# Weights' low parts subtracted in pieces on GpSimd, and inverse norms left in PSUM, in a hybrid HGRN and attention layer

## The chip, the cores and the metric

The kernel runs on one core of a Trainium2 chip. The metric is the device time of one launch in microseconds (us). A core has TensorE (PE; its weight loads are listed as PEld), VectorE (DVE), ScalarE (ACT), GpSimd (POOL) and SyncE (SP), which issues the DMAs here. Each engine works through its own instructions in order and waits on semaphores for the others.

## The reference

One step of a layer in which two groups of heads work side by side, for a prompt of 2048 tokens and a sample of 32 tokens with a cache of 256. Cut to what matters:

```
h = rms_norm(x, norm1);  z = h @ w_in            # 1024 -> 3592 columns
# HGRN2: 4 heads of 128, chunks of 64
f = lb + (1 - lb) * sigmoid(fa);  k = 1 - f;  b = cumsum(log f)
o = (q*exp(b)) @ S0 + tril((q*exp(b-bref)) @ (k*exp(bref-b)).T) @ v
S = exp(b_last) * S0 + (k*exp(b_last-b)).T @ v
oa = rms_norm_per_head(o) * silu(ga)             # the "inverse norm of the HGRN output"
# FoX attention: 8 heads of 64
fq = rms_norm(qb, q_gain);  fk = rms_norm(kb, k_gain)   # the "inverse norm of Q"
p = softmax(fq @ fk.T / 8 + sum of log forget, causal);  ob = p @ v
x = x + concat(oa, ob) @ w_out
x = x + square(relu(rms_norm(x, norm2) @ w_up)) @ w_down
```

All of it is in float32.

## The kernel before

The prompt is worked on in four quarters of 512 tokens; the sample's 32 tokens ride with the third (544 columns, done as two of 272). A float32 product is made of three matmuls in a faster format: each operand is split into a high part (a rounded copy) and a low part (what is left), and high by high, high by low and low by high are summed in PSUM (`mm3`).

A weight comes in blocks of 128 x 1024 numbers, 384 of them in the launch. `load_w` loads one (L161, on SyncE), makes the high part `wh` on ScalarE (L163) and the low part `wl` on GpSimd (L165). Each of the three has two buffers. A strip of the projection is such a block of `w_in`; `strip` runs it over the quarters that are ready, and hands each result to an evacuation.

What happens between the strips is laid out at build time: `Flow` keeps a clock of the matmuls emitted and steps side jobs (generators) as their due times come, so that TensorE's order is a dense stream of strips with small jobs in between: `finish` of K, V and Q, the tails of HGRN, attention. A scheduler below the program places the instructions on their engines and adds the waits.

The steps that the change touches:

- `squares` puts the squares of x and their high and low parts into SBUF: product and subtraction on GpSimd (L287, L291), the copy on ScalarE (L289).
- In `fox_q`, `norm` sums them over the 64 rows of a head with two matmuls against ones (`tq`), in a PSUM tile of `ps_tr`. `inv_norm` makes exp(-0.5 ln(mean + eps)) with Ln (L279) and Exp (L280) into an SBUF tile, and VectorE multiplies Q by it and by the gain (L485). Ahead of L493 and L495, which split the result.
- In HGRN's `i_tail` the same is done for the output: matmuls (`th`), Ln (L762), Exp over all columns (L763), product on VectorE (L764). L790 to L794 follow in `g_tail`.
- `ps_tr` has two buffers, in turn. All transposes use it too: `ta` (activations), `tk`, `tv`, `th`, `mt`, `tg`, `tl`, `ts`.

Lines of VectorE that are named below and not changed: L247 (a row times its inverse norm and the gain), L429 and L430 (K times its inverse norm, times the gain), L634 to L647 (nine small products and copies that scale HGRN's queries and keys), L843 and L844 (high and low part of the attention's row maxima), L723 (the HGRN state), L883 (low part of attention weights, one operand in PSUM), L905, L916 and L920 (the end of a head's attention), L528 (the high part of V).

From some 1100 us on the kernel is in its second half: output projections, the second norm, and the feed-forward of one quarter after the other, with the attention of the later quarters beside it.

Of the kernel before, what the change touches and what calls it, by code (L numbers as in the profile page):

```python
# [9 lines left out]
F32 = mybir.dt.float32  # L10
# [3 lines left out]
AF = mybir.ActivationFunctionType  # L14
ALU = mybir.AluOpType
# [4 lines left out]
P = 128  # L20
# [55 lines left out]
def hymba_step(  # L76
# [8 lines left out]
    pe, act, dve, pool, sp = nc.tensor, nc.scalar, nc.vector, nc.gpsimd, nc.sync  # L85
# [8 lines left out]
    def mm(out, lhsT, rhs, start, stop):  # L94
        n = rhs.free_size()
        if rhs.dtype == F32:
            flow.t += max(n, 32) * 4 * 0.00042
        else:
            flow.t += n * 0.00042 if n >= 256 else 0.213
        pe.matmul(out, lhsT, rhs, start=start, stop=stop)  # L100

    def tp(out, in_, idn):
        flow.t += 0.109
        pe.transpose(out, in_, idn)  # L104
# [53 lines left out]
    def load_w(src, kt, ncols, pfx):  # L158

        raw = wpool.tile([P, kt, ncols], F32, tag="wraw", name=f"wr{pfx}", bufs=2)  # L160
        sp.dma_start(raw, src.rearrange("(k p) c -> p k c", p=P))  # L161
        hi = wpool.tile([P, kt, ncols], F32R, tag="whi", name=f"wh{pfx}")
        act.copy(hi, raw)  # L163
        lo = wpool.tile([P, kt, ncols], F32R, tag="wlo", name=f"wl{pfx}")
        pool.tensor_tensor(lo, raw, hi.bitcast(F32), op=ALU.subtract)  # L165
        return hi, lo

    def mm3(out, wh, wl, ah, al, kts):
# [10 lines left out]
    def nid():  # L179
        uid[0] += 1  # L180
        return uid[0]
# [93 lines left out]

    def inv_norm(ss, cnt):

        t = tt([P, 544])[:, 0:ss.free_size()]
        act.activation(t, ss, AF.Ln, scale=1.0 / cnt, bias=epsc)  # L279
        act.activation(t, t, AF.Exp, scale=-0.5)  # L280
        return t

    def squares(x):

        n = x.free_size()
        sq = tt([P, 544])[:, 0:n]
        pool.tensor_tensor(sq, x, x, op=ALU.mult)  # L287
        sh = tt([P, 544], F32R)[:, 0:n]
        act.copy(sh, sq)  # L289
        sl = tt([P, 544], F32R)[:, 0:n]  # L290
        pool.tensor_tensor(sl, sq, sh.bitcast(F32), op=ALU.subtract)  # L291
        return sh, sl
# [5 lines left out]
    def tt(shape, dt=F32, tag="t", bufs=None):  # L298
        return tmp.tile(shape, dt, tag=tag, name=f"{tag}{nid()}", bufs=bufs)

    def strip(col, A, qs, evac):
        hi, lo = load_w(w_in[:, col:col + P], KT, P, nid())
        for q in qs:
            ah, al = A[q]
            for c0, n in QCH[q]:
                ps = ps_mm.tile([P, 512], F32, tag="mm", name=f"mm{nid()}")
                yield from mm3(ps[:, 0:n], lambda k: hi[:, k, :], lambda k: lo[:, k, :],
                               lambda k: ah[:, k, c0:c0 + n], lambda k: al[:, k, c0:c0 + n],
                               [(k, k) for k in range(KT)])
                g = evac(q, c0, n, ps)  # L310
                if g is not None:
                    flow.spawn(g, SL)
                yield
# [253 lines left out]
    def hgrn(A, qs, h):  # L567
# [132 lines left out]
        def i_tail(q, d, z):  # L700
            vp = ps_tr.tile([P, 4, P], F32, tag="tr", name=f"th{nid()}")
            for i in range(4):
                tp(vp[:, i, :], z[:, i * P:(i + 1) * P], ident)
            v = tt([P, 544])
            act.copy(v[:, 0:512], vp.rearrange("p i k -> p (i k)"))
            v = v[:, 0:512].rearrange("p (i k) -> p i k", k=P)
            yield 1.0
            while "kt" not in d or (q > 0 and h_done[h] != q):
                yield 0.5
            kt_ = d["kt"][:, 0:512].rearrange("p (i k) -> p i k", k=P)  # L710
            up = ps_x.tile([P, 4, P], F32, tag="x", name=f"xu{nid()}")
            for i in range(4):
                mm(up[:, i, :], kt_[:, i, :], v[:, i, :], start=True, stop=True)
            us = tt([P, 544])[:, 0:512].rearrange("p (i k) -> p i k", k=P)
            act.copy(us, up)
            yield 0.3
            op = ps_x.tile([P, 4, P], F32, tag="x", name=f"xo{nid()}")
            QE, at, dec = d["QE"], d["at"], d["dec"]
            for i in range(4):
                mm(op[:, i, :], S_cur[h], QE[:, i * P:(i + 1) * P], start=True, stop=False)  # L720
                mm(op[:, i, :], v[:, i, :], at[:, i, :], start=False, stop=True)
                sn = tmp.tile([P, P], F32, tag=f"S{h}", name=f"S{h}_{nid()}", bufs=2)
                dve.scalar_tensor_tensor(out=sn, in0=S_cur[h], scalar=dec[:, i:i + 1], in1=us[:, i, :],  # L723
                                         op0=ALU.mult, op1=ALU.add)
                S_cur[h] = sn
                yield 0.6
            h_done[h] += 1
            at_busy[q % 2] = False
            o = tt([P, 544])
            act.copy(o[:, 0:512], op.rearrange("p i k -> p (i k)"))  # L730
            if q == 3:
                sp.dma_start(ns_p[0, 0, h], S_cur[h])
            if QN[q] > 512:
                yield 0.5
                ec = d["ec"]
                vp = ps_tr.tile([P, 512], F32, tag="tr", name=f"th{nid()}")
                tp(vp[0:TS, 0:P], z[:, 512:544], ident)
                vs = tt([TS, P], tag="vts", bufs=1)
                act.copy(vs, vp[0:TS, 0:P])
                s0 = tt([P, P], tag="s0", bufs=1)  # L740
                sp.dma_start(s0, state_hgrn[0, 0, h])
                yield 3.0
                xp_ = ps_x.tile([P, 512], F32, tag="x", name=f"xu{nid()}")
                mm(xp_[:, 0:P], d["kts"], vs, start=True, stop=True)
                mm(xp_[:, P:P + TS], s0, QE[:, 512:544], start=True, stop=False)
                mm(xp_[:, P:P + TS], vs, d["ats"], start=False, stop=True)
                sn = tt([P, P], tag="sn", bufs=1)
                dve.scalar_tensor_tensor(out=sn, in0=s0, scalar=ec[:, 2, 8:9], in1=xp_[:, 0:P],
                                         op0=ALU.mult, op1=ALU.add)
                sp.dma_start(ns_s[0, 0, h], sn)  # L750
                act.copy(o[:, 512:544], xp_[:, P:P + TS])

            n = QN[q]
            sh, sl = squares(o[:, 0:n])
            yield HLAT
            r = tt([P, 544])
            for c0, w in ((0, 512), (512, TS))[0:1 + (n > 512)]:
                c = slice(c0, c0 + w)
                ss = ps_tr.tile([P, 512], F32, tag="tr", name=f"th{nid()}")
                mm(ss[:, 0:w], oner, sh[:, c], start=True, stop=False)  # L760
                mm(ss[:, 0:w], oner, sl[:, c], start=False, stop=True)
                act.activation(r[:, c], ss[:, 0:w], AF.Ln, scale=1.0 / P, bias=epsc)  # L762
            act.activation(r[:, 0:n], r[:, 0:n], AF.Exp, scale=-0.5)  # L763
            dve.tensor_tensor(o[:, 0:n], o[:, 0:n], r[:, 0:n], op=ALU.mult)  # L764
            d["o"] = o

        def evac_g(q, c0, n, ps):
# [42 lines left out]
    cnt = {"kb0": 0, "kb1": 0, "qc": 0}  # L810
# [234 lines left out]
    def add_tokens(acc, ah, al, w, evac=None):  # L1045

        for hf in range(2):
            c = slice(512 * hf, 512 * hf + 512)
            hi, lo = load_w(w[:, c], 2, 512, nid())
            for t in range(4):  # L1050
                ts = slice(t * P, (t + 1) * P)
                ps = ps_mm.tile([P, 512], F32, tag="mm", name=f"mm{nid()}")
                yield from mm3(ps, lambda k: ah(k)[:, ts], lambda k: al(k)[:, ts],
                               lambda k: hi[:, k, :], lambda k: lo[:, k, :], [(0, 0), (1, 1)])
                dve.tensor_tensor(acc[:, t, c], acc[:, t, c], ps, op=ALU.add)  # L1055
                if evac is not None:
                    flow.spawn(evac(t, c), 1.5)
                yield
# [185 lines left out]
    epsc = const.tile([P, 1], F32, name="epsc")  # L1244
# [29 lines left out]
    for i in range(4):  # L1274
        t = const.tile([98, 512], F32R, name=f"kB{i}")
# [5 lines left out]
    for i in range(2):  # L1281
        t = const.tile([98, 512], F32R, name=f"qC{i}")
# [15 lines left out]
    for i in range(2):  # L1298
        t = tmp.tile([P, 4, P], F32, tag=f"AT{i}", name=f"AT{i}", bufs=1)
# [94 lines left out]
```

## Time and profile before

| | |
|---|---|
| time, median of 3 runs | 2978.21 us (2977.03 to 2981.14) |
| the profiled execution | 2982.22 us; span of its instructions 2980.5 us |
| mean granted TensorE clock | 0.990 |
| PE | busy 2875.0 us (96%), 15592 matmuls |
| DVE | busy 1840.9 us (62%), 3463 instructions |
| ACT | busy 1368.4 us (46%), 2391 instructions |
| POOL | busy 1091.2 us (37%), 600 instructions, of which L165 934.2 us |

Busy time of DVE and POOL counts from an instruction's start to its end, whatever it does in between. Matmuls overlap, so that a stall of TensorE is read better from the starts of consecutive matmuls than from its busy share.

### The profile page before, as it was taken

The page shows a single profiled execution, that of the slowest core. Times are in us where ns is not written, and L with a number is a line of the kernel's source. Part 1 is how long each engine was busy: PE and PEld are TensorE (multiplying, and loading weights), DVE is VectorE, ACT ScalarE, POOL GpSimd, SP SyncE. Part 2 cuts the span into 40 slices and gives each one's busy share as a digit, 9 for nine tenths or more (in the row PEclk, how much of TensorE's full clock was granted, in tenths as well). Part 3 has the DMA queues.
Part 4 walks back from the last instruction along what each step waited for, and adds up shares of the span by engine and source line. Part 5 has one row for each costly group of instructions (what it writes and reads, how often), then busy time and mean ns, then how long its engine had stood idle before and what let it go on. Part 6 is the DMA issues. An engine that isn't in the chain of part 4 may idle for free.

```text
span 2980.5 us, 42522 instructions
## 1 busy us (share of the span) xinstructions
PE 2875.0 (96%) x15592; PEld 2435.9 (82%) x15592; DVE 1840.9 (62%) x3463; ACT 1368.4 (46%) x2391; POOL 1091.2 (37%) x600
## 2 busy tenths in 40 slices
PE   6899999899999999999999999999999999999999
PEld 5777777877788878888888888978899989988887
DVE  6447778776876777766666666566666554444333
ACT  4445566655555554544444444454444433222232
POOL 5452233434112334433333333333333344344443
PEclk9899999999999999999999999999999999999999
DMA  5663344656433564344335633443633333243333
GB/s 163 186 187 87 102 121 117 179 156 186 116 102 89 162 202 128 110 121 119 114 123 156 189 112 112 130 141 111 185 108 109 93 103 93 86 129 107 96 95 99
DMA packets 464143, 381.86 MB, mean 128 GB/s; under 512 B 34928, under 2 KB 363904, under 8 KB 463936
## 3 DMA queue, kind: packets, MB, share of 16 engines
q1 hardware_dynamic: 463936, 379.15, 43.6%
q8 instruction: 123, 2.02, 0.3%
q14 instruction: 84, 0.69, 0.1%
HBM read 316.67 MB, written 62.40 MB: 127 GB/s over the span
## 4 chain that ended last, share of the span: by engine, by line
PE 62%; DVE 1%; ACT 1%; issue 0%; POOL 0%; DMA 0%; SPq 0%; DVEq 0%; ACTq 0%; POOLq 0%
PE mm L100 54%; PE ot L100 3%; PE st L100 3%; PE mx L100 1%; PE ta L104 0%; PE rs L100 0%; ACT wh L163 0%; DMA row<-X 0%; DVE acc L1055 0%; PE tx L104 0%; POOL wl L165 0%; PE ty L104 0%; DVE os L916 0%; DVE ml L920 0%; DVE row L247 0%
## 5 line engine op out<-in xcount | busy, mean ns | idle before, releaser
L165 POOL TENSOR_TENSOR wl<-wr,wh 128x1024 fp32r<-128x1024 f32 x384 | 934.2, 2433 | 1685.7 <-ACT wh L163 1483.0
L100 PE MATMUL mm<-ahi,wh 128*128 128x512 f32 (+1 forms) x2528 | 899.0, 356 | 2.9 <-ACT t L512 1.6
L100 PE MATMUL mm<-ahi,wl 128*128 128x512 f32 (+1 forms) x2528 | 884.9, 350 | 1.5 <-POOL wl L165 1.5
L100 PE MATMUL mm<-alo,wh 128*128 128x512 f32 (+1 forms) x2528 | 885.8, 350 | 0.0
L163 ACT CAST wh<-wr 128x1024 fp32r<-128x1024 f32 x384 | 403.5, 1051 | 745.0 <-PE mm L100 645.3
L100 PEld LDWEIGHTS mm<-ahi,wh 128*128 128x128 f32 x2528 | 481.0, 190 | 63.2 <-DVE t L621 2.6
L100 PEld LDWEIGHTS mm<-ahi,wl 128*128 128x128 f32 x2528 | 479.7, 190 | 62.2 <-POOL wl L165 1.9
L100 PEld LDWEIGHTS mm<-alo,wh 128*128 128x128 f32 x2528 | 480.9, 190 | 57.3 <-issue 0.5
L1055 DVE TENSOR_TENSOR acc<-acc,mm 128x512 f32<-128x512 f32 x480 | 326.1, 683 | 155.7 <-PE mm L100 150.1
L879 ACT ACTIVATE st<-st 128x512 f32<-128x512 f32 (+1 forms) x320 | 169.3, 529 | 351.1 <-PE st L100 188.7
L883 DVE TENSOR_TENSOR pl<-st,ph 128x512 fp32r<-128x512 f32 (+1 forms) x320 | 198.2, 620 | 198.0 <-ACT ph L881 196.6
L100 PE MATMUL mm<-wh,uh 128*128 128x512 f32 x768 | 306.9, 400 | 2.8 <-DVE acc L1055 1.6
L100 PE MATMUL mm<-wh,ul 128*128 128x512 f32 x768 | 302.7, 395 | 0.0
L100 PE MATMUL mm<-wl,uh 128*128 128x512 f32 x768 | 302.5, 394 | 0.0
L1115 DVE TENSOR_TENSOR mm<-mm,r 128x512 f32<-128x512 f32 (+1 forms) x160 | 95.8, 599 | 291.0 <-ACT r L1114 289.1
L839 DVE TENSOR_REDUCE mc<-mx 128x1 f32<-128x512 f32 (+2 forms) x320 | 195.7, 617 | 36.9 <-PE mx L100 34.5
L100 PEld LDWEIGHTS mm<-wh,uh 128*128 128x128 f32 x768 | 144.6, 188 | 41.3 <-DVE acc L1055 7.5
L100 PEld LDWEIGHTS mm<-wh,ul 128*128 128x128 f32 x768 | 144.8, 189 | 35.2 <-DVE ul L1117 0.2
L887 DVE TENSOR_TENSOR acc<-acc,st 128x512 f32<-128x512 f32 (+2 forms) x288 | 173.3, 602 | 0.0
L881 ACT CAST ph<-st 128x512 fp32r<-128x512 f32 (+1 forms) x320 | 169.8, 532 | 7.2
L100 PEld LDWEIGHTS mm<-wl,uh 128*128 128x128 f32 x768 | 144.8, 189 | 30.8
L100 PE MATMUL mm<-uh,wh 128*128 128x272 f32 x512 | 149.6, 292 | 1.3 <-DVE acc L1148 1.3
(296 smaller groups left out, 4275.6 us busy)
## 6 DMA issues: line engine op xcount, KB each, us to landing
wr<-in_w_up_dram SPq DMA_DIRECT2D x128, 512.0 KB
wr<-in_w_down_dram SPq DMA_DIRECT2D x128, 512.0 KB
wr<-in_w_in_dram SPq DMA_DIRECT2D x96, 512.0 KB
kB<-KS SPq DMA_DIRECT2D x160, 128.0 KB
kA<-KS SPq DMA_DIRECT2D x80, 256.0 KB
V<-VS SPq DMA_DIRECT2D x80, 256.0 KB
wr<-in_w_out_dram SPq DMA_DIRECT2D x32, 512.0 KB
out_dram<-t SPq DMA_DIRECT2D x32, 256.0 KB
```

The source lines that it names most:

```text
L100: pe.matmul(out, lhsT, rhs, start=start, stop=stop)
L163: act.copy(hi, raw)
L165: pool.tensor_tensor(lo, raw, hi.bitcast(F32), op=ALU.subtract)
L839: dve.tensor_reduce(out=mc[:, j, kb:kb + 1], in_=mx[:, 0:n], axis=AX.X, op=ALU.max)
L879: act.activation(st[:, off:], st[:, off:], AF.Exp)
L881: act.copy(ph[:, off:], st[:, off:])
L883: dve.tensor_tensor(pl[:, off:], st[:, off:], ph.bitcast(F32)[:, off:], op=ALU.subtract)
L887: dve.tensor_tensor(acc[:, off:], acc[:, off:], st[:, off:], op=ALU.add)
L1055: dve.tensor_tensor(acc[:, t, c], acc[:, t, c], ps, op=ALU.add)
L1115: dve.tensor_tensor(z, z, r, op=ALU.mult)
```

## The change

The subtraction that makes a weight's low part is done in four instructions of 256 columns each instead of one of 1024; its operands are seen as flat rows of 1024. `inv_norm` writes its Ln and Exp over the sums, in the PSUM tile where the matmuls left them, and returns that tile; `norm` multiplies Q by it from there. The HGRN output's norm calls `inv_norm` too, for each range of columns (512, and in the third quarter another 32), and multiplies each range by the PSUM tile.

```diff
@@ load_w
         act.copy(hi, raw)
         lo = wpool.tile([P, kt, ncols], F32R, tag="wlo", name=f"wl{pfx}")
-        pool.tensor_tensor(lo, raw, hi.bitcast(F32), op=ALU.subtract)
+
+        fl = lambda a: a.rearrange("p k c -> p (k c)")
+        for c in range(0, kt * ncols, 256):
+            s = slice(c, c + 256)
+            pool.tensor_tensor(fl(lo)[:, s], fl(raw)[:, s], fl(hi.bitcast(F32))[:, s], op=ALU.subtract)
         return hi, lo
@@ inv_norm
-        t = tt([P, 544])[:, 0:ss.free_size()]
-        act.activation(t, ss, AF.Ln, scale=1.0 / cnt, bias=epsc)
-        act.activation(t, t, AF.Exp, scale=-0.5)
-        return t
+        act.activation(ss, ss, AF.Ln, scale=1.0 / cnt, bias=epsc)
+        act.activation(ss, ss, AF.Exp, scale=-0.5)
+        return ss
@@ i_tail
-            r = tt([P, 544])
             for c0, w in ((0, 512), (512, TS))[0:1 + (n > 512)]:
                 c = slice(c0, c0 + w)
                 ss = ps_tr.tile([P, 512], F32, tag="tr", name=f"th{nid()}")
                 mm(ss[:, 0:w], oner, sh[:, c], start=True, stop=False)
                 mm(ss[:, 0:w], oner, sl[:, c], start=False, stop=True)
-                act.activation(r[:, c], ss[:, 0:w], AF.Ln, scale=1.0 / P, bias=epsc)
-            act.activation(r[:, 0:n], r[:, 0:n], AF.Exp, scale=-0.5)
-            dve.tensor_tensor(o[:, 0:n], o[:, 0:n], r[:, 0:n], op=ALU.mult)
+                r = inv_norm(ss[:, 0:w], P)
+                dve.tensor_tensor(o[:, c], o[:, c], r, op=ALU.mult)
```

## Rows read from the trace of the kernel before

**Rows 1.** Busy us of each engine, granted clock and DMA, in two stretches.
```profile
core 0: us, PE busy (x) PEld busy (x) DVE busy (x) ACT busy (x) POOL busy (x), PEclk, DMA share, GB/s
0.00:1200.00 1200.00, 1104.96 (x6176) 915.26 (x6177) 847.24 (x1691) 661.89 (x1273) 419.31 (x289) 0.98 0.50 143
1200.00:2981.00 1781.00, 1770.03 (x9417) 1520.66 (x9415) 993.65 (x1773) 706.51 (x1118) 671.85 (x311) 1.00 0.40 118
```

**Rows 2.** Four VectorE lines: duration ns min/median/max, first and last start us, forms.
```profile
L485 DVE SCALAR_TENSOR_TENSOR t<-t,qg,t x20: 215/746/2960, 74.6 to 773.0; 128x512 f32<-128x512 f32 x16, 128x32 f32<-128x32 f32 x4
...
L429 DVE TENSOR_TENSOR t<-t,krs x20: 281/1174/2883, 46.0 to 742.9; 128x512 f32<-128x512 f32 x16, 32x128 f32<-32x128 f32 x4
...
L634 DVE COPY hcc<-he x16: 150/160/2361, 222.6 to 1052.2; 128x4 f32<-128x4 f32 x16
...
L883 DVE TENSOR_TENSOR pl<-st,ph x320: 391/681/693, 247.9 to 2394.0; 128x512 fp32r<-128x512 f32 x128, 128x256 fp32r<-128x256 f32 x32
```

**Rows 3.** Timeline about 600 us: start us, us, instruction [idle before <- ended by].
```profile
599.32 2.39 POOL L165 TENSOR_TENSOR wl<-wr,wh 128x1024 fp32r<-128x1024 f32 x1 [2.03 <-ACT wh L163]
...
599.73 2.52 DVE L485 SCALAR_TENSOR_TENSOR t<-t,qg,t 128x512 f32<-128x512 f32 x1
...
601.20 0.29 PE L100 MATMUL mm<-alo,wh 128*128 128x272 f32 x1
602.91 0.38 PE L100 MATMUL mx<-kB,qC 96*128 96x256 f32 x1 [1.42 <-DVE mc L839]
```

**Rows 4.** Timeline of TensorE: the first and the last of 59 stalls.
```profile
28.24 0.42 PE L100 MATMUL mm<-alo,w 128*40 128x512 f32 x1 [0.35 <-DVE alo L198]
...
1153.27 0.47 PE L100 MATMUL mm<-wh,ahi 128*128 128x512 f32 x1 [1.42 <-DVE acc L1055]
```

**Rows 5.** Stretches of low clock, first and last of ten; columns as in rows 1.
```profile
74.70:81.60 6.90, 5.58 (x15) 4.55 (x16) 3.72 (x8) 2.66 (x5) 0.00 (x0) 0.51 0.84 246
...
1037.30:1040.70 3.40, 3.40 (x13) 2.81 (x12) 2.73 (x9) 2.03 (x4) 0.00 (x0) 0.50 1.04 249
```

**Rows 6.** Two GpSimd lines; columns as in rows 2.
```profile
L165 POOL TENSOR_TENSOR wl<-wr,wh x384: 2340/2403/3459, 24.1 to 2965.5; 128x1024 fp32r<-128x1024 f32 x192
...
L291 POOL TENSOR_TENSOR t<-t,t x32: 1266/1302/1843, 55.7 to 1080.2; 128x512 fp32r<-128x512 f32 x24, 128x544 fp32r<-128x544 f32 x8
```

**Rows 7.** GpSimd's lines by shape: busy us, mean ns, idle before and its releasers.
```profile
L165 POOL TENSOR_TENSOR wl<-wr,wh 128x1024 fp32r<-128x1024 f32 x384 | 934.2, 2433 | 1685.7 <-ACT wh L163 1483.0 <-PE st L100 49.7 <-PE ot L100 33.4
L291 POOL TENSOR_TENSOR t<-t,t 128x512 fp32r<-128x512 f32 x24 | 32.5, 1356 | 18.6 <-ACT t L289 17.9 <-DMA KS<-t 0.7
```

**Rows 8.** Timeline of the feed-forward stage: a subtraction and the first load of its result.
```profile
2709.77 2.42 POOL L165 TENSOR_TENSOR wl<-wr,wh 128x1024 fp32r<-128x1024 f32 x1 [3.96 <-ACT wh L163]
...
2714.22 0.19 PEld L100 LDWEIGHTS mm<-ahi,wl 128*128 128x128 f32 x1
```

**Rows 9.** Waits: engine and line <- what ended them: us in total, times, longest.
```profile
PE mm L100 <- POOL wl L165: 2.7, 2, 1.5
...
ACT wh L163 <- DMA wr<-in_w_in_dram: 8.6, 4, 3.4
```

**Rows 10.** Timeline of GpSimd and VectorE at three places where their instructions meet.
```profile
24.13 5.70 POOL L165 TENSOR_TENSOR wl<-wr,wh 128x1024 fp32r<-128x1024 f32 x2
...
24.20 3.39 DVE L247 SCALAR_TENSOR_TENSOR row<-row,rs,gbc 128x1024 f32<-128x1024 f32 x1
...
364.25 3.40 POOL L165 TENSOR_TENSOR wl<-wr,wh 128x1024 fp32r<-128x1024 f32 x1 [1.82 <-ACT wh L163]
...
364.74 0.68 DVE L641 TENSOR_TENSOR t<-t,hcc 128x512 f32<-128x512 f32 x1
...
1055.09 2.56 POOL L165 TENSOR_TENSOR wl<-wr,wh 128x1024 fp32r<-128x1024 f32 x1
...
1055.34 2.85 DVE L641 TENSOR_TENSOR t<-t,hcc 128x512 f32<-128x512 f32 x1
```

**Rows 11.** Timeline about 565 us: a norm of Q and the next transposes.
```profile
564.89 0.69 ACT L279 ACTIVATE t<-tq,epsc 128x512 f32<-128x512 f32 x1
...
565.71 0.60 PE L104 MATMUL tk<-identr,t 128*128 128x128 f32 x4
...
567.29 0.74 DVE L485 SCALAR_TENSOR_TENSOR t<-t,qg,t 128x512 f32<-128x512 f32 x1
```

## The prediction

> **What bounds the kernel now.** I read the page's busy shares first, then two stretches side by side, then the waits, then single stalls in the timeline. The stretches [rows 1] split the kernel. From 1200 us on TensorE is busy 1770 of 1781 us, so nothing done on another engine can give more than 11 us there. In the first 1200 us (projections, HGRN, the start of attention) it is busy 1105, and its granted clock is 0.98: about 95 us of idleness and 24 us of clock are to be had, and only there.
>
> What TensorE waits for in that stretch is mostly VectorE, and VectorE is late for a reason that the durations show [rows 2]. L485 takes 746 ns at the median and 2960 at most, L429 1174 and 2883, and L634, a copy of four columns, 160 and 2361. L883, of the same size but with one operand in PSUM, stays between 391 and 693 over 320 instructions. The timeline says what the long ones have in common [rows 3]: L485 starts at 599.73 while GpSimd's L165 runs from 599.32 to 601.71, and it ends at 602.25: less its usual 0.75, it began at 601.5, when GpSimd was done. TensorE pays: after 601.20 its next matmul comes at 602.91, 1.71 us later where its neighbours are 0.13 apart. A VectorE instruction with two SBUF operands (or a plain copy) waits for GpSimd's instruction to end; one with an operand in PSUM does not. [...]
>
> I followed every TensorE stall of over 0.15 us in the first 1200 us back along VectorE's and ScalarE's queues, up to 12 us. 59 stalls have a blocked VectorE instruction behind them; each counted for no more than the block, they make 60.5 us. The first and the last are in [rows 4]; the last follows L920, blocked behind L165. [...]
>
> **The change, part by part.**
>
> *The subtraction in four pieces.* Before, L165 takes 2403 ns at the median for 1024 columns. The nearest row is the same subtraction on 512 columns, 1302 ns at the median [rows 6]: 2.15 ns a column and 201 ns fixed. A piece of 256 is then 0.55 + 0.20 = 0.75 us, four are 3.0, and a weight's low part is ready 0.6 us later. Bounds: no fixed cost at all, 2.4 (later by 0); by the means of lines by shape, where L165 is 2433 and L291 1356 [rows 7], 0.82 a piece and 3.3 (later by 0.9). I take 0.6, near the medians, which are free of blocks. GpSimd goes from 1091 to some 1320 us, 44%, and does not become the bound.
>
> What covers the 0.6: in the feed-forward stage L165 ends at 2712.19 and the weight load that first wants it starts at 2714.22 [rows 8], 2.0 us of cover, and the last pieces are wanted only later in the strip. The wait on that load is met long before, and the load takes its 0.19 us; three more such waits for each weight I cost at nothing. TensorE waited for L165 twice in the first 1200 us, 2.7 us in all [rows 9]; with pieces the first is there 1.6 us sooner, which I leave out. The raw weights' buffer comes free 0.6 later, so SyncE, in order, issues that load and what is queued behind it 0.6 later; ScalarE's cast waited for such a load (of w_in) 4 times, 8.6 us [rows 9], and not all of them were TensorE's loss, so I take nothing (bound: 4 times 0.6).
>
> [...] Three cases are in [rows 10]. [...] At 1055.09 L165 waits for a running VectorE instruction, goes first, and the next one, L641 at 1055.34, waits out all of it. But L165 at 364.25 takes 3.40: there L641 at 364.74, right behind another VectorE instruction, went ahead of it. [...] L287 and L291 on GpSimd stay whole, and stalls behind them stay.
>
> Of the 60.5 us: 8.7 us (nine stalls, the first that of [rows 3]) stand behind a blocked L485 or L764, and 16.2 behind HGRN's run of nine contending instructions (L634 to L647). The other 35.6 are behind lone or paired ones (L429 with L430, L843 with L844, L723, L920, L528) or behind L287 and L291. I take 8 of the first back, 7 of the second (between none and two thirds) and 20 of the third (a block of 2.2 falls to between 0.75 and 1.5): 35 us. Of the clock's 25.6 I take 10, since the stalls that start a low stretch are the long ones and some only shrink.
>
> *The inverse norms in PSUM.* ScalarE does the same Ln and Exp, with four short instructions more in HGRN, and VectorE four short products more, some 2 us of engines that have room. Reading PSUM, L883 is no slower than 693 ns [rows 2]. [...]
>
> The price is the PSUM tile, of which there are two. Before, it is free when Ln has read it; now it is held through Exp and the product. At 564.89 L279 starts and ends at 565.58, and transposes into the next tile but one start at 565.71, while the product ends only at 568.03 [rows 11]. They would wait, in TensorE's order, with all matmuls behind them; 1.6 us if ScalarE and VectorE come to the two steps sooner, 2.3 if not. I went through the 40 norms: in five the next tile but one is wanted before the product ends (by 0.5 us or less in three). I take 4 us. Bounds: 0, if the order gives way, and 60, if all 40 paid 1.5.
>
> **The sum.** The profiled execution is 2982.2 us (span 2980.5). 2982.2 - 35 - 10 + 4 = 2941. The median of the runs is 4.0 below the profiled one: **2937 us**, 1.4% faster.
>
> **The rivals.**
>
> *Nearly all the blocking goes* (chance 0.17). [...]
>
> *The pieces hand nothing over* (0.12). If GpSimd's four follow so closely that VectorE gets in only after the last, a block grows from 2.4 to 3.0, and only the PSUM operands help: -8.7, -2 of clock, +4, and some 0.2 for each of 30 other stalls, +6: 2978 us, no change. The case at 24.20 speaks against it.
>
> *The held PSUM tile decides* (0.13). Every norm's tile is wanted by a dense stream of transposes; if 30 of the 40 pay 1.5 to 2.3, say 57 us, against a gain of 45, the time is 2990 us, slower. It decides from some 24 stalls of 1.9 us on. In the trace of before it is 5 of 40, but with less waiting TensorE comes to the next transposes sooner.
>
> **How the numbers follow.** The forecast has 0.58, its own range 2916 to 2958: 22 us of saved stall and 6 of clock at one end, 50 and 16 at the other. The whole range, 2897 to 2981, leaves out most of the slow case and half of the big gain. Under 0.2% (6 us) a measurement can't tell from no change. Faster: 0.58 + 0.17 + a little of the third, 0.77. Same: 0.10. Slower: 0.13.
>
> **What would show it.** L485 and L764 never over 0.9 us. L165 four times as many, each 0.6 to 0.8 us. The longest L429, L634, L843 and L920 under 1.7 us; VectorE's busy time down by 50 to 90 us. TensorE's idle time in the first 1200 us down by a third, with fewer stretches at 0.5. After that, TensorE at the same rate. Wrong would be: long L429 as before (no handover), or transposes (tk, ta, th, mt) that wait for L485 or L764; or the instructions in another order on VectorE, which would move stalls by amounts that the trace of before can't tell.

## The result, and the profile after

The changed kernel takes 2944.3 us (median of 4 runs, 2944.19 to 2944.37) against 2979.7 before: a ratio of 0.9882, 95% interval 0.9865 to 0.9899. It is 1.2% faster; 2937 was forecast, 1.4%, and the range held it. The profiled execution took 2944.2 us, with a span of 2942.5. The lines of the code shift by one to four: the subtraction is now L169, the product of Q L488, that of HGRN's norm L765, K's first product L432, HGRN's run of small instructions L637 to L650.

The two stretches first, with the columns of [rows 1]:

```profile
0.00:1200.00 1200.00, 1127.87 (x6367) 938.85 (x6368) 832.02 (x1745) 685.21 (x1325) 513.09 (x661) 0.99 0.51 146
1200.00:2942.50 1742.50, 1731.76 (x9227) 1489.35 (x9225) 950.71 (x1723) 681.11 (x1071) 768.97 (x1091) 1.00 0.40 118
```

TensorE's idle time in the first 1200 us falls from 95 us to 72, and its granted clock rises from 0.98 to 0.99. After 1200 us it has 10.7 us of idleness, where [rows 1] had 11: the gain lies wholly in the first stretch, as its idle time did.

Now the VectorE instructions that GpSimd held, with the columns of [rows 2] (minimum, median, maximum in ns). "Held" means that an instruction lasts longer than the shortest of its line and shape. [rows 2] has the first, third and fourth of these as they were; the product of HGRN's norm was, before:

```profile
L764 DVE TENSOR_TENSOR t<-t,t x16: 669/688/2598, 271.5 to 1086.7; 128x512 f32<-128x512 f32 x12, 128x544 f32<-128x544 f32 x4
```

And after:

```profile
L488 DVE SCALAR_TENSOR_TENSOR t<-t,qg,tq x20: 239/734/749, 71.4 to 731.8; 128x512 f32<-128x512 f32 x16, 128x32 f32<-128x32 f32 x4
...
L765 DVE TENSOR_TENSOR t<-t,th x20: 172/676/690, 258.4 to 1048.2; 128x512 f32<-128x512 f32 x16, 128x32 f32<-128x32 f32 x4
...
L432 DVE TENSOR_TENSOR t<-t,krs x20: 278/934/1220, 44.9 to 707.3; 128x512 f32<-128x512 f32 x16, 32x128 f32<-32x128 f32 x4
...
L637 DVE COPY hcc<-he x16: 151/164/700, 212.3 to 1013.5; 128x4 f32<-128x4 f32 x16
```

The maximum is the column to read. The two products with an operand in PSUM never exceed 749 ns, where they reached 2960 and 2598: they aren't held at all. K's product and the copy of four columns, which still read SBUF alone, go from 2883 and 2361 to 1220 and 700: they are held for one piece and no longer for a whole subtraction. The median of the copy, 164 where it was 160, doesn't tell this, since nine of its 16 instances meet no GpSimd instruction.

Counted over every VectorE instruction (duration over the shortest of its line and shape, where that is over 0.15 us), the held time is 130.9 us in 101 instructions before and 70.4 us in 147 after. Before, 46 were held for more than 1.5 us; after, one. More instructions are held, each for less.

The groups by line, with the columns of [rows 7], give the other side:

```profile
L169 POOL TENSOR_TENSOR wl<-wr,wh 128x256 fp32r<-128x256 f32 x1536 | 1130.7, 767 | 1471.0 <-ACT wh L163 1361.3 <-DMA wr<-in_w_up_dram 19.8 <-PE mm L100 19.7
```

GpSimd pays 1131 us for its subtractions where it paid 934, and stays idle more than half of the span (busy 1282 of 2942.5 us).

How VectorE and GpSimd take turns is seen in the timeline where a run of VectorE instructions meets the four pieces:

```profile
226.44 2.91 POOL L169 TENSOR_TENSOR wl<-wr,wh 128x256 fp32r<-128x256 f32 x4 [8.07 <-ACT wh L163]
...
227.29 0.71 DVE L844 CAST mpad<-nm 128x4 fp32r<-128x4 f32 x1
...
227.92 0.15 DVE L639 TENSOR_TENSOR hcc<-he 128x4 f32<-128x4 f32 x1
...
228.00 0.69 DVE L640 COPY hcc<-he 128x4 f32<-128x4 f32 x1
228.60 0.15 DVE L845 TENSOR_TENSOR mpad<-nm,mpad 128x4 fp32r<-128x4 f32 x1
228.68 0.69 DVE L641 TENSOR_TENSOR hcc<-he 128x4 f32<-128x4 f32 x1
...
228.90 0.40 PE L104 MATMUL mt<-identr,mpad 128*2 128x128 f32 x4 [0.64 <-DVE mpad L845]
```

Three instructions that need some 0.16 us (L844, L640, L641) end at 228.00, 228.69 and 229.37: 0.69 apart, about a piece's length. Behind each of the first two another one (L639, L845) still gets through, and ends 0.07 us later; the one after that waits out the next piece. So two of VectorE's small instructions get through at each turn here, not a whole run; the engines take turns. TensorE waits 0.64 us at this place. Shorter GpSimd instructions give more turns, and the maxima above fall with them, from 2883 and 2361 ns to 1220 and 700.

It isn't always so. In the same timeline at 444 us one row product waits out all four pieces:

```profile
444.27 2.78 POOL L169 TENSOR_TENSOR wl<-wr,wh 128x256 fp32r<-128x256 f32 x4
444.33 3.80 DVE L251 SCALAR_TENSOR_TENSOR row<-row,rs,gbc 32x1024 f32<-32x1024 f32 x1 [0.97 <-POOL rs L156]
...
448.78 0.38 PE L100 MATMUL mx<-kB,qC 96*128 96x256 f32 x1 [3.13 <-DVE mc L840]
```

It usually takes 1.27 us; it ends at 448.13, so it began at 446.86 (the pieces run to 447.05 in the trace, 0.19 later: the two times agree no better than that). This is the one block of over 1.5 us that is left, and it costs TensorE 3.1 us. The start 0.06 us after the first piece doesn't explain it: nine other instructions that GpSimd's own results released, eight of L432 and one of L251, all on 128 rows, started 0.07 us after a first piece and were held for that piece alone (L432 took 1.21 to 1.22 us). In the kernel with the pieces only three started 0.01 to 0.05 us after one and were held no longer either. This one works on the sample's 32 rows. Why it got no turn isn't shown.

The price of the held PSUM tile shows as transposes that wait for a product:

```profile
71.40 0.73 DVE L488 SCALAR_TENSOR_TENSOR t<-t,qg,tq 128x512 f32<-128x512 f32 x1
...
72.19 0.66 PE L104 MATMUL ta<-identr,row 128*128 128x128 f32 x4 [2.28 <-DVE t L488]
...
1048.15 0.68 DVE L765 TENSOR_TENSOR t<-t,th 128x512 f32<-128x512 f32 x1
...
1048.98 0.47 PE L100 MATMUL mm<-wh,ahi 128*128 128x512 f32 x1 [1.46 <-DVE t L765]
```

These two and one of 0.55 us at 463.4 are all: 4.7 us beyond TensorE's usual step.

The first and the last of the eight stretches of low clock in the first 1200 us, with the columns of [rows 5]:

```profile
22.80:26.20 3.40, 3.09 (x10) 1.85 (x11) 3.40 (x5) 1.90 (x3) 3.33 (x4) 0.50 0.01 2
...
1060.50:1067.30 6.80, 6.06 (x14) 4.51 (x15) 3.77 (x6) 1.80 (x3) 0.76 (x2) 0.50 1.04 390
```

Over the span there are ten such stretches, at a granted clock of 0.50, where before there were 14; that at 353.9 follows 3.6 us in which TensorE waited for VectorE (L886), and that at 449.5 the 3.1 us of the row product above.

**The accounts.** I followed TensorE's stalls back as the prediction did, now over the whole span. A stall is what a matmul's step exceeds the usual one of its shape by, over 0.15 us where VectorE or ScalarE ended it, over 0.4 us where GpSimd did. The clock's cost is the length of each stretch of low granted clock times what is missing from 1, as the trace records it. All in us; V/S stands for VectorE or ScalarE; "held" is the part of the VectorE and ScalarE stalls that a held VectorE instruction accounts for; the last column is the span less stalls and clock.

| kernel | median (ratio, interval) | span | V/S stalls | held part | GpSimd | clock | rest |
|---|---|---|---|---|---|---|---|
| before | 2979.7 | 2980.5 | 104.6 | 63.4 | 6.0 | 32.2 | 2837.7 |
| after | 2944.3 (0.9882) | 2942.5 | 81.9 | 32.7 | 3.4 | 22.1 | 2835.1 |
| pieces only | 2953.1 (0.9916, 0.9901 to 0.9930) | 2951.6 | 83.8 | 36.8 | 3.5 | 28.9 | 2835.4 |
| PSUM only | 2970.9 (0.9971, 0.9962 to 0.9981) | 2977.0 | 100.2 | 58.0 | 5.7 | 33.5 | 2837.6 |
| 2 x 512 | 2963.3 (0.9949, 0.9934 to 0.9964) | 2960.6 | 93.4 | 47.2 | 3.6 | 29.8 | 2833.8 |
| 8 x 128 | 2951.2 (0.9910, 0.9895 to 0.9925) | 2949.8 | 81.0 | 26.0 | 3.7 | 30.9 | 2834.2 |
| 16 x 64 | 3005.6 (1.0084, 1.0069 to 1.0099) | 3001.6 | 117.4 | 10.1 | 10.3 | 37.5 | 2836.4 |
| no subtraction | 2884.5 (0.9679, 0.9663 to 0.9695) | 2883.7 | 38.7 | 4.6 | 1.1 | 8.4 | 2835.5 |
| squares halved | 2947.0 (0.9890, 0.9875 to 0.9904) | 2946.8 | 79.8 | 32.0 | 3.4 | 27.1 | 2836.5 |
| powers on ScalarE | 2935.7 (0.9848, 0.9832 to 0.9865) | 2939.1 | 68.2 | 24.1 | 3.7 | 30.4 | 2836.8 |
| K from PSUM | 2948.8 (0.9899, 0.9885 to 0.9914) | 2952.7 | 80.8 | 28.8 | 3.4 | 31.2 | 2837.3 |
| both of these | 2923.2 (0.9807, 0.9793 to 0.9822) | 2921.5 | 60.7 | 23.2 | 3.5 | 22.0 | 2835.3 |
| another order | 2948.3 (0.9895, 0.9880 to 0.9909) | 2946.2 | 79.9 | 27.6 | 3.4 | 27.6 | 2835.3 |

The last column is 2833.8 to 2837.7 in all of them, while the span moves by 118 us: what TensorE does besides is the same everywhere, and whatever a variant gains or loses is in its stalls and in the clock. Part of this is bookkeeping, since stalls and clock are taken off the same span, and the table alone doesn't say why a stall arose. The held part is the held time found on the way back, at most the stall itself; a clock that is low after a stall isn't split by the stall's cause. Each experiment below is read by these columns. The span is that of one profiled execution; the medians are within 7 us of it.

### The profile page after: what moved, and what is told of

The parts are those of the page before. It is cut to its first block, busy times and chain, and to the rows that moved or that the text cites. A ratio compares the mean times of both kernels' runs of the same rounds, so it can differ in the third digit from the quotient of the medians.

```text
span 2942.5 us, 43855 instructions
## 1 busy us (share of the span) xinstructions
PE 2859.6 (97%) x15592; PEld 2428.2 (83%) x15592; DVE 1782.7 (61%) x3467; ACT 1366.3 (46%) x2395; POOL 1282.1 (44%) x1752
## 4 chain that ended last, share of the span: by engine, by line
PE 63%; DVE 1%; ACT 1%; DMA 0%; issue 0%; POOL 0%; SPq 0%; ACTq 0%; POOLq 0%; DVEq 0%
PE mm L100 55%; PE ot L100 3%; PE st L100 3%; PE mx L100 1%; PE ta L104 1%; DMA row<-X 0%; PE rs L100 0%; PE tx L104 0%; DMA acc<-in_x_prompt_dram 0%; PE ty L104 0%; ACT wh L163 0%; POOL wl L169 0%; DVE row L251 0%; DVE acc L1056 0%; DVE pl L884 0%
## 5 line engine op out<-in xcount | busy, mean ns | idle before, releaser
L169 POOL TENSOR_TENSOR wl<-wr,wh 128x256 fp32r<-128x256 f32 x1536 | 1130.7, 767 | 1471.0 <-ACT wh L163 1361.3
L840 DVE TENSOR_REDUCE mc<-mx 128x1 f32<-128x512 f32 (+2 forms) x320 | 195.8, 618 | 34.9 <-PE mx L100 32.5
```

The costliest lines, as they stand in the source:

```text
L169: pool.tensor_tensor(fl(lo)[:, s], fl(raw)[:, s], fl(hi.bitcast(F32))[:, s], op=ALU.subtract)
L840: dve.tensor_reduce(out=mc[:, j, kb:kb + 1], in_=mx[:, 0:n], axis=AX.X, op=ALU.max)
```

## The experiments

All but the first start from the changed kernel. Theory A is the prediction's: VectorE's instructions are held for one GpSimd instruction, and TensorE waits behind them.

**The two halves apart.** The kernel before with the four pieces alone:

```diff
-        pool.tensor_tensor(lo, raw, hi.bitcast(F32), op=ALU.subtract)
+        for c in range(0, kt * ncols, 256):
+            s = slice(c, c + 256)
+            pool.tensor_tensor(fl(lo)[:, s], fl(raw)[:, s], fl(hi.bitcast(F32))[:, s], op=ALU.subtract)
```

> The subtraction in four pieces alone; inverse norms in SBUF as before. Theory A (VectorE's contending instructions wait for GpSimd's running instruction, so the length of that instruction is what matters): most of the gain, L485 and L764 blocked for at most 0.8 us instead of 2.4, no transposes waiting for the norm's product; 2940 to 2955 us. Rival B (the gain comes from the other order in which the scheduler below the program put the instructions once durations changed): any time from 2940 to 2985, not ordered by the length of the pieces over the runs of this set.

Its product of Q (L489):

```profile
L489 DVE SCALAR_TENSOR_TENSOR t<-t,qg,t x20: 214/762/1226, 72.8 to 746.9; 128x512 f32<-128x512 f32 x16, 128x32 f32<-128x32 f32 x4
```

With both operands in SBUF the product of Q is held, but for half a microsecond instead of 2.2. And the changed kernel with the subtraction whole again (L484 is the product of Q, L428 that of K):

> The inverse norms in PSUM alone; the subtraction in one instruction of 1024 columns. Theory A: the products of Q and of the HGRN output never over 0.8 us, but L429 still up to 2.9 and L634 up to 2.4; about 9 us of stall goes, 4 to 5 us come back through transposes that wait for the product: 2968 to 2980 us. Rival B: not told.

```profile
L484 DVE SCALAR_TENSOR_TENSOR t<-t,qg,tq x20: 235/740/748, 73.6 to 764.8; 128x512 f32<-128x512 f32 x16, 128x32 f32<-128x32 f32 x4
...
L428 DVE TENSOR_TENSOR t<-t,krs x20: 278/693/2871, 45.7 to 737.5; 128x512 f32<-128x512 f32 x16, 32x128 f32<-32x128 f32 x4
```

Here one product is free and the other still held for 2.2 us. Against the runs of before beside them (2980.7) the pieces give 27.6 us and the PSUM operands 9.8, in sum 37.4, where both together give 35.4: within the noise the halves add up. The profiled execution of the second was the longest of its ten (2978.7), so its row in the table understates it.

**The length of a piece.** Two pieces of 512, eight of 128, sixteen of 64:

```diff
-        for c in range(0, kt * ncols, 256):
-            s = slice(c, c + 256)
+        for c in range(0, kt * ncols, 512):       # then 128, then 64
+            s = slice(c, c + 512)
```

> The changed kernel with two pieces of 512 columns. Theory A: the longest block about 1.3 us, so a gain between that of no pieces (about 2974) and that of four (2944): 2952 to 2968 us. Rival C (TensorE or the loads profit from the first piece being ready sooner, not VectorE from short blocks): as with four pieces, 2941 to 2948 us.

> The changed kernel with eight pieces of 128 columns, by the rows 0.47 us each, 3.8 us a weight against 2.95 with four. Theory A: the longest block about 0.5 us, but runs of contending VectorE instructions may meet more pieces: 2928 to 2945 us. Rival C: as with four pieces or later by the longer sum, 2943 to 2955 us.

> The changed kernel with sixteen pieces of 64 columns, by the rows 0.33 to 0.34 us each, 5.4 us a weight, against 5.4 to 5.6 us that TensorE spends on a weight in the feed-forward stage. Theory A: the blocks are short, but GpSimd has no room left there: TensorE waits for the low parts, 2950 to 3060 us, with waits of TensorE for the subtraction in the waits' list. If GpSimd's fixed cost hides behind the piece before, no such wait and 2930 to 2945 us.

The groups by line of the three kernels, in this order:

```profile
L169 POOL TENSOR_TENSOR wl<-wr,wh 128x512 fp32r<-128x512 f32 x768 | 1003.3, 1328 | 1599.5 <-ACT wh L163 1480.9 <-PE st L100 31.8 <-PE mm L100 16.4
```
```profile
L169 POOL TENSOR_TENSOR wl<-wr,wh 128x128 fp32r<-128x128 f32 x3072 | 1379.0, 486 | 1249.5 <-ACT wh L163 1180.8 <-PE mm L100 16.7 <-DMA MTH<-t 11.9
```
```profile
L169 POOL TENSOR_TENSOR wl<-wr,wh 128x64 fp32r<-128x64 f32 x6144 | 1845.7, 343 | 862.5 <-ACT wh L163 859.7 <-ACT th L283 2.8
```

The held part falls all the way, 58.0, 47.2, 32.7, 26.0, 10.1 from the whole to 64 columns: theory A in its plainest form. Rival C, the first piece being ready sooner, is ruled out by the two pieces: they gave 2963.3, where it said 2941 to 2948. But from 256 to 128 the total of the stalls hardly moves, 81.9 and 81.0, and at 64 it is 117.4, because the others rise: total less held is 42.2, 46.2, 49.2, 55.0 and 107.3. By GpSimd's busy time a weight's subtraction takes 2.43 us whole, 2.61 in two, 2.94 in four, 3.59 in eight and 4.81 in sixteen. The waits of the last kernel say who is late:

```profile
DVE row L251 <- POOL rs L156: 55.0, 17, 9.8
DVE t L432 <- POOL krs L156: 50.5, 18, 4.7
...
PEld mm L100 <- POOL wl L169: 6.1, 6, 1.5
```

VectorE's waits for the norms of rows (rs) and of K (krs), which GpSimd makes between the subtractions in its own order, total 31.3 and 37.8 us with 256 columns, and TensorE begins to wait for the low parts themselves. That last wait, which the expectation named, is the small part: the stalls behind GpSimd grow from 3.4 to 10.3 us, those not tied to a held instruction from 49.2 to 107.3. Eight pieces missed theory A's expectation by 6 us, and 2951.2 lies in rival C's range: against four, 6.7 us of held stalls less are met by 5.8 of others, and the clock takes 8.8 more. The waits for rs and krs grow by only 4.9 us there (36.6 and 37.4), so that the queue shows clearly with sixteen pieces alone; with eight, most of the loss is the clock's, which another order of instructions moves too (by 5.5 us, below). Theory A has no term for the queue.

**No subtraction.** The low parts aren't made; the high part stands in for them, so TensorE does the same work on other numbers.

```diff
-        lo = wpool.tile([P, kt, ncols], F32R, tag="wlo", name=f"wl{pfx}")
...
-        return hi, lo
+        return hi, hi
```

> The changed kernel without the subtraction: the weights' low parts are not made, and the high part stands in their place in every matmul, so the same matmuls run on other numbers. Theory A: no VectorE instruction waits for a weight any more, only for the squares' two GpSimd instructions: most of the 33 us of stall that still had a blocked instruction behind it in the changed kernel and some of the clock go, 2905 to 2928 us. [...]

The first 1200 us of it, columns as in [rows 1]:

```profile
0.00:1200.00 1200.00, 1164.70 (x6594) 972.00 (x6595) 814.99 (x1805) 708.29 (x1360) 142.04 (x189) 1.00 0.54 151
```

TensorE is idle for 35 us there and its granted clock is 1.00. The kernel gains 60 us over the changed one, 20 more than the largest gain expected. The accounts split it: 28.1 us of held stalls (32.7 to 4.6), 15.1 of other stalls (49.2 to 34.1), 13.7 of clock and 2.3 of GpSimd's own. So held instructions account for about half of what the subtractions cost, and for some three fifths of the stalls that go; the clock's part isn't split between the two kinds of stall. VectorE's waits for krs and rs fall by 9.6 us (to 30.4 and 29.1), so that GpSimd's lateness is a candidate for the other stalls. Most of those waits, though, are there without any subtraction: GpSimd's own work on the norms is slow (its power on 128x8 takes 1.64 us at the mean in the changed kernel).

**The squares in halves too.** GpSimd's other long instructions, which the change left whole:

```diff
-        pool.tensor_tensor(sl, sq, sh.bitcast(F32), op=ALU.subtract)
+        for c in (0, h):
+            pool.tensor_tensor(sl[:, c:c + h], sq[:, c:c + h], sh.bitcast(F32)[:, c:c + h], op=ALU.subtract)
```

(and the same for the square itself.)

> The changed kernel with the two GpSimd instructions of the squares (product, subtraction) each done in two halves. Theory A: the blocks behind them, up to 1.1 us in the changed kernel, halve, and the 4.5 us stall near 127 us shrinks; against it, the squares come 0.2 to 0.4 us later: 2936 to 2946 us.

2947.0 us, no gain, and 1 us outside what was expected: the held part falls by 0.7 us, all stalls by 2.1, and the clock takes 5.0 more. What was left behind the squares was small.

**The queue by itself.** If GpSimd's lateness counts, the inverse norms should pay when another engine makes them. Logarithm and exponential on ScalarE in the place of GpSimd's power:

```diff
-        pool.tensor_scalar(out, ss, 1.0 / cnt, EPS, op0=ALU.mult, op1=ALU.add)
-        pool.tensor_tensor(out, out, phalf[0:out.shape[0], 0:n], op=ALU.pow)
+        act.activation(out, ss, AF.Ln, scale=1.0 / cnt, bias=epsc[0:out.shape[0]])
+        act.activation(out, out, AF.Exp, scale=-0.5)
...
-            pool.tensor_tensor(r[0:w, :], ss[0:w, 0:1], ss[0:w, 1:2], op=ALU.add)
+            dve.tensor_tensor(r[0:w, :], ss[0:w, 0:1], ss[0:w, 1:2], op=ALU.add)
```

> The changed kernel, but the inverse norms of the rows and of K's rows are raised to the power -1/2 on ScalarE (logarithm, then exponential) and no longer on GpSimd, and the sum of the two partial squares is made on VectorE; the small constant that goes in is made at the start. [...] Rival D (what the kernel without subtractions gained beyond the blocked stalls is GpSimd being late with the norms that VectorE and TensorE wait for): VectorE's waits for krs (37.8 us) and rs (31.3 us) go to a fraction, 2925 to 2938 us.

The waits of this kernel:

```profile
DVE t L432 <- ACT krs L156: 16.2, 11, 2.9
...
DVE rs L249 <- ACT junk L246: 12.1, 4, 5.2
...
DVE row L251 <- ACT rs L156: 3.9, 6, 1.3
```

37.8 and 31.3 us became 16.2 and 3.9; against that, VectorE makes the sum itself now and waits 12.1 us for ScalarE's squares, as GpSimd did before. The time is 2935.7, within what rival D gave; theory A by itself, by which this edit changes nothing but the order, had 2940 to 2948. Rival D fits as a second part beside theory A; the gain of 8.6 us is twice what another order moves below, and with the next edit added it is larger (2923.2 us, below). Of the 13.7 us of stalls that go, 8.6 are held ones, though VectorE is held for as long as before: 68.7 us in 152 instructions, against 70.4 in 147. Less of it reaches TensorE; that VectorE comes to its work sooner would explain it, and wasn't tested by itself. (Its profiled execution was the longest of four, 2941.2, so its row in the table understates it.)

**K's product from PSUM.** The one frequent product that was still held:

```diff
-            act.copy(kn, tr)
...
-            dve.tensor_tensor(k3, k3, r.unsqueeze(2).to_broadcast([w, g, DH]), op=ALU.mult)
+            dve.tensor_tensor(k3, tr.rearrange("p (g d) -> p g d", d=DH), r.unsqueeze(2).to_broadcast([w, g, DH]), op=ALU.mult)
```

> The changed kernel, with K's first product reading K from the transposes' PSUM tile instead of a copy in SBUF, so that ScalarE's copy falls away and VectorE's instruction has one operand less in SBUF. Theory A (an instruction of VectorE that reads PSUM isn't held by GpSimd): K's product is never over 1.3 us, ScalarE has some 20 copies fewer, and the tile is held a little longer: 2935 to 2945 us. Rival (the held tile decides): TensorE's transposes of the rows wait for the tile, over 2948 us.

Its product (L431), and who waited for it in us and times:

```profile
L431 DVE TENSOR_TENSOR t<-tk,krs x20: 279/692/692, 46.4 to 718.7; 128x512 f32<-128x512 f32 x16, 32x128 f32<-32x128 f32 x4
...
  PE tq L100: 3.6, 2
  PE ta L104: 1.8, 2
```

Not one of the 20 is held, and yet the time is 2948.8: theory A's range is missed, and the rival's (over 2948) just met. The tile is now held until GpSimd has made krs, and TensorE waits for it four times, 5.4 us. With both edits together:

> Both edits at once: norms' powers on ScalarE, and K's product from PSUM. By theory A with rival D as a second part, the two gains add up: 2918 to 2935 us. If the first two runs of this call gain nothing, this gains nothing.

```profile
L431 DVE TENSOR_TENSOR t<-tk,krs x20: 278/691/694, 45.4 to 686.1; 128x512 f32<-128x512 f32 x16, 32x128 f32<-32x128 f32 x4
...
  PE tv L104: 0.3, 1
```

ScalarE makes krs in two instructions of 0.3 and 0.2 us, where GpSimd's power alone takes 1.64 on 128x8 (mean in the changed kernel); the tile comes free sooner and the 5.4 us are 0.3. The pair takes 2923.2 us, 21 us less than the changed kernel, where the single edits gave 8.6 and minus 4.5: more than their sum, and 8.4 us of the step from the first edit alone are the clock's by the table. It is the fastest complete version here, 1.9% below the kernel before (0.9793 to 0.9822).

**Another order.** Stalls depend on which instructions happen to meet. One constant of the plan that places the side jobs, from 4.5 to 4.6, adds and removes nothing:

```diff
-    KLAT, QLAT, HLAT, SL = 9.0, 8.0, 7.0, 4.5
+    KLAT, QLAT, HLAT, SL = 9.0, 8.0, 7.0, 4.6
```

> The changed kernel with one constant of the plan at 4.6 instead of 4.5: no instruction is added or removed, only the order of side jobs shifts. Theory A: within 5 us of the changed kernel, 2939 to 2949 us. Rival B (the gain of the change is mostly luck of the order): 10 us or more to either side.

2948.3 us, 4.0 more than the changed kernel. Its held part is 5.1 us smaller, its other stalls 3.1 greater, its clock 5.5 dearer. So differences of 4 us between variants, such as those of the halved squares and of K's product alone, aren't to be read as causes, and with one other order tried, the 7 us between four and eight pieces aren't safe either; 35 us are. Rival B, that the gain is luck of the order, said 10 us or more here.

## Why the prediction was right, step by step

- **Where the time is to be had:** right. The gain is in the first 1200 us; the second stretch kept its rate.
- **The stalls behind held instructions, 35 of 60.5 us:** too much by a fifth. In the first 1200 us they fall to 32.5, 28.0 us less; 30.7 over the whole span. By the prediction's classes: those behind L485 and L764 go to nothing (8 of 8.7 were counted), HGRN's run goes from 16.2 to 12.9 where 7 were counted, the others from 35.6 to 19.6, 16 where 20 were counted. HGRN's term is the one most out of proportion, 3.3 for 7: where VectorE's instructions alternate with the pieces, as at 228 us, a run pays for several of them, which is near the lower end of the prediction's "between none and two thirds". The 0.75 to 1.5 us taken for a block of the others rests on VectorE getting in between two queued GpSimd instructions; the trace of before showed it at 24.13 us [rows 10], where two L165 take 5.70 us, 0.9 more than twice their median of 2.40, and L247, which needs some 1.27, ends at 27.59 between them. The stall at 393.2 us, 1.9 us, has six instructions held for some 0.5 us each behind it. The handover itself, on which the rival "the pieces hand nothing over" turned, is shown by the 45 fewer long blocks.
- **The clock, 10 us:** 32.2 to 22.1 over the span, 10.1. The 25.6 us that it was taken from are ten stretches of the trace of before ([rows 5] has the first and the last), 51.1 us in all at a granted clock of 0.50 to 0.51. The size is partly luck. Of the kernels with the same four pieces and stalls of 80 to 84 us, pieces only, squares halved, K from PSUM and the other order pay 27 to 31; the change is worth 1 to 10 us here, by the order.
- **A piece of 0.75 us, four 3.0:** 0.74 at the median (0.767 at the mean), 2.94 for four. The cover held: the two waits of TensorE for the low part, 2.7 us, are gone, as the first piece is there sooner; that was left out.
- **The held PSUM tile, 4 us:** 4.7 in three places. In the changed kernel the rival "the held PSUM tile decides" came nowhere near its 24 stalls. The sign of being wrong, transposes that wait for these products, did show, at the size that the sum had counted. A kernel that held a tile for GpSimd did pay it (K's product, alone).
- **PSUM operands cost nothing:** right. On 128x512 the shortest L488 takes 724 ns, where the shortest L485 took 742, and L765 666, where L764 took 669. The prediction's row for this, L883, mixes shapes: its instances on 128x512 take 657 to 693 ns, and the 391 is of 128x256.
- **GpSimd doesn't become the bound:** its 1282 us are 44% of the span, but a step is missing here. VectorE's waits for rs and krs, made in GpSimd's order, grew from 21.5 and 33.9 us to 31.3 and 37.8, and the stalls not tied to held instructions from 41.2 to 49.2. The held tile is 4.7 of these 8.0; the other 3.3 were not foreseen. It took sixteen pieces to make the step large; with the powers on ScalarE more than half of these waits went.
- **The sum.** Forecast: -35 - 10 + 4 = -41. Measured on the spans: -30.7 held, +8.0 other stalls, -2.6 waits for GpSimd, -10.1 clock and -2.6 rest, together -38.0. The held stalls and the others came out 8.3 us worse than forecast, and the waits for GpSimd and the rest, which the forecast had at nothing, gave 5.2 back: that the sum misses by only 3 is partly luck. The other 4 us of the miss are the difference between the profiled execution of before and its median, which the forecast carried over; after, the profiled execution is the median. The upper end of the prediction's own range doesn't follow from its terms: 22 us of stall and 6 of clock, with 4 for the tile, give 2954, not 2958. The result lies inside either.
- **VectorE's busy time:** down by 58 us, within the 50 to 90 given. The longest L432, L637, L844 and L921 are 1.22, 0.70, 0.71 and 1.22 us, all under 1.7; the one long block that is left, L251 at 444 us, wasn't on that list. TensorE's idle time fell by a quarter where a third was said.

## What to carry to other kernels

Where VectorE and GpSimd work at the same time, look at the maximum of a VectorE line beside its median (2960 ns and 746 for the product of Q before the change), and ask what TensorE waits for behind the long ones: cutting the GpSimd instruction bounds the wait to about one piece at most places (one long block of 46 was left here), and moving an operand to PSUM ends it (749 ns at most for the two products here). Cut only as far as GpSimd's own queue allows, since what it makes between the pieces comes later (VectorE's waits for rs and krs went from 55.4 us to 69.1), and move its small urgent products to another engine if they come late (cutting further after that wasn't tried). A tile that is held for a slow producer takes back what the freed instruction gave (5.4 us with K's product); make the producer fast first.

## What the runs showed of the hardware

A GpSimd subtraction has a fixed cost: means of 2.43, 1.33, 0.77, 0.49 and 0.34 us for 1024, 512, 256, 128 and 64 columns, so that 1024 numbers a row keep GpSimd busy for 4.81 us in pieces of 64, where one instruction takes 2.43. GpSimd's power on 128x8 takes 1.64 us (mean of 16); ScalarE's logarithm and exponential for the same norms take 0.30 and 0.20 (medians).

With the pieces queued behind one another VectorE got its turn at each end of a piece at 228 us, and at 444 us a VectorE instruction waited out all four. In the runs with pieces, the same happened to a product on the sample's 32 rows that GpSimd's own norm had released 0.05 to 0.06 us after the first piece began, with two pieces (3.53 us at 455), eight (4.38 at 447), the halved squares (3.81 at 448), K's product from PSUM (3.81 at 452) and the other order (K's product on 32 rows, 3.94 at 568). With sixteen pieces that row product was held for little (1.41 us at 466), but a copy of 128x320 that needs 0.32 us took 3.85 at 30 us. In the two kernels with the powers on ScalarE, where GpSimd releases neither product, it didn't happen, and in that with the pieces only no such start occurs. What decides between a turn and none isn't settled.
